# Strassen's seven products in place of eight for the second feed-forward projection, six blocks of eight, summed in DRAM

## The chip, the cores and the metric

The kernel runs on one core of one Trainium2 chip. The metric is the device time of one execution in microseconds (us). A core has five engines that run beside each other, each through its own list of instructions in order: TensorE (PE in the profile), VectorE (DVE), ScalarE (ACT), GpSimd (POOL) and SyncE (SP). Here SP and POOL only issue transfers (DMA).

## The reference

One layer of a diffusion transformer with 512 tokens and a model width of 2048. The part around the change is the feed-forward half:

```python
D_MODEL, SEQ, D_FF = 2048, 512, 8192

def sq_relu_mlp(h, w1, b1, w2, b2):
    return jnp.square(jax.nn.relu(h @ w1 + b1)) @ w2 + b2
...
    h2 = modulate(x, sh2, sc2)
    x = layer_norm(DEEPNORM_ALPHA * x + g2 * sq_relu_mlp(h2, w_ff1, b_ff1, w_ff2, b_ff2), ln2_g, ln2_b)
```

`h @ w1` is 512x2048 by 2048x8192, and the second product 512x8192 by 8192x2048. All inputs and the output are float32.

## The kernel before

The first half of the kernel (input projection, attention, convolution, output projection, first layer norm) is not touched. It leaves `h2`, transposed, and the residual stream `res[t][i]`: four tiles of 128 tokens, each in two halves of 1024 columns.

**Three matmuls for each product.** Each float32 operand is converted into a rounded high part and a low part that holds the rest (`split`): ACT writes the high part, then DVE subtracts it from the source. `mm3` multiplies high by high, high by low and low by high. A tile of weights, 128x1024, is loaded by SP into one of four tiles of `rpool` (tag `R`) and converted by `wsplit` into a pair `wh`, `wl`. The pairs live in slots that `turn["w"]` hands out in rotation, three in the feed-forward half: two of `wpool`, one of `xw`. A conversion must wait until PE is done with the slot's old weights, and for DVE's half also until ACT's half is written.

**Eight blocks.** The hidden width of 8192 is worked off in eight blocks `q` of 1024, and each block has two stages:

- the first projection, `hidden(n, ...)`, for eight groups `n` of 128 hidden columns: two tiles of weights, 48 matmuls (tile `f`), then ReLU with bias on ACT, the square on DVE, and a `split` into `fh`, `fl`. All are 512 tokens wide, except in block 0, which does the tokens in two halves.
- the second projection, `down(q, c, ...)`, for four groups `c` of 512 output columns: four tiles of weights, 96 matmuls into four PSUM banks (tile `d`, one for each 128 tokens). Then DVE multiplies each bank by the gate `g2` and adds it into `res` (`add_gated`).

```python
                for t in range(4):
                    mm3(ps[t], hi[:, s, sl], lo[:, s, sl], wh[:, s * 512:(s + 1) * 512], wl[:, s * 512:(s + 1) * 512],
                        j == j0 and s == 0, j == j1 - 1 and s == 1)
        for t in range(4):
            add_gated(g2, ps[t], t, c)
```

The hidden part is the operand that PE holds (128x128), the weights are the one that streams past it (512 columns). Block 7 does the last half of its second projection token by token, with the last layer norm and the stores behind it. The bias `b_ff2`, times the gate, is added to `res` by `bias2`, whose steps run between the groups of block 1 (`side.step`).

A scheduler sets the order of instructions on each engine when the program is built, from the order of the code, and it chooses the slots. At run time each engine keeps to its list: an instruction that waits holds up all that stand behind it on the same engine. `upool` has 30 tiles of 128x1024; 16 of them hold `h2` in the feed-forward half.

## Time and profile before

| | |
|---|---|
| time, median of 3 runs | 2460.5 us (2457.34 to 2461.24) |
| profiled execution, its own time | 2461.58 us |
| its span, first to last instruction | 2459.8 us |
| mean granted clock of TensorE | 0.996 |
| PE busy | 2405.3 us, 98% of the span, 11764 matmuls |
| DVE busy | 1368.6 us, 56% |
| ACT busy | 788.2 us, 32% |

The profile is one execution on the chip. The granted clock is the share of TensorE's full clock that the chip let it have. "Busy" counts the time in which an engine has an instruction under way; matmuls overlap their successors, so a busy PE says nothing on its pace, which is read from the starts of its matmuls. Idle time of an engine matters only where the last work to end waits for it.

### The profile page before, as it was taken

The page shows a single profiled execution, that of the slowest core. Times are in us where ns is not written, and L with a number is a line of the kernel's source. Part 1 is how long each engine was busy: PE and PEld are TensorE (multiplying, and loading weights), DVE is VectorE, ACT ScalarE, POOL GpSimd, SP SyncE. Part 2 cuts the span into 40 slices and gives each one's busy share as a digit, 9 for nine tenths or more (in the row PEclk, how much of TensorE's full clock was granted, in tenths as well). Part 3 has the DMA queues.
Part 4 walks back from the last instruction along what each step waited for, and adds up shares of the span by engine and source line. Part 5 has one row for each costly group of instructions (what it writes and reads, how often), then busy time and mean ns, then how long its engine had stood idle before and what let it go on. Part 6 is the DMA issues. An engine that isn't in the chain of part 4 may idle for free.

```text
span 2459.8 us, 29177 instructions
## 1 busy us (share of the span) xinstructions
PE 2405.3 (98%) x11764; PEld 1921.1 (78%) x11764; DVE 1368.6 (56%) x1870; ACT 788.2 (32%) x1109; POOL 51.8 (2%) x100
## 2 busy tenths in 40 slices
PE   6999999999989999999999999999999999999998
PEld 4777777777678888898888888888888888888886
DVE  4556999934767777854554433434334334334368
...
GB/s 331 243 219 188 183 221 217 278 271 263 268 207 201 166 106 199 60 155 146 120 137 94 96 99 96 95 95 94 94 95 96 101 95 94 94 94 94 98 123 106
DMA packets 109463, 371.01 MB, mean 151 GB/s; under 512 B 13064, under 2 KB 19592, under 8 KB 109328
## 3 DMA queue, kind: packets, MB, share of 16 engines
...
## 4 chain that ended last, share of the span: by engine, by line
PE 89%; issue 4%; DMA 3%; ACT 2%; DVE 2%; POOL 0%; SPq 0%; DVEq 0%; ACTq 0%; POOLq 0%
PE f L119 9%; PE f L118 9%; PE f L117 9%; PE d L119 9%; PE d L118 9%; PE d L117 9%; PE u L117 3%; PE u L118 2%; PE u L119 2%; PE gb L217 2%; PE v L117 2%; PE v L119 2%; PE v L118 2%; PE o L578 1%; PE s L556 1%
## 5 line engine op out<-in xcount | busy, mean ns | idle before, releaser
L104 DVE TENSOR_TENSOR wl<-w,wh 128x1024 fp32r<-128x1024 f32 x262 | 320.3, 1224 | 679.2 <-ACT wh L103 679.2
L103 ACT ACTIVATE wh<-w 128x1024 fp32r<-128x1024 f32 x262 | 277.3, 1060 | 901.8 <-PE d L119 502.3
L119 PE MATMUL f<-h2h,wl 128*128 128x512 f32 (+1 forms) x1152 | 424.5, 369 | 3.7 <-DVE wl L104 3.7
L117 PE MATMUL f<-h2h,wh 128*128 128x512 f32 (+1 forms) x1152 | 423.9, 368 | 0.1
L118 PE MATMUL f<-h2l,wh 128*128 128x512 f32 (+1 forms) x1152 | 423.6, 368 | 0.0
L119 PE MATMUL d<-wh,fl 128*128 128x512 f32 x960 | 379.7, 395 | 0.0
L118 PE MATMUL d<-wl,fh 128*128 128x512 f32 x960 | 376.6, 392 | 0.0
L117 PE MATMUL d<-wh,fh 128*128 128x512 f32 x960 | 374.9, 391 | 0.0
L119 PEld LDWEIGHTS f<-h2h,wl 128*128 128x128 f32 x1152 | 218.0, 189 | 41.3 <-DVE wl L104 4.3
L117 PEld LDWEIGHTS f<-h2h,wh 128*128 128x128 f32 x1152 | 218.2, 190 | 37.5 <-ACT wh L103 0.3
L118 PEld LDWEIGHTS f<-h2l,wh 128*128 128x128 f32 x1152 | 217.9, 189 | 37.2
L118 PEld LDWEIGHTS d<-wl,fh 128*128 128x128 f32 x960 | 180.3, 188 | 43.8
L117 PEld LDWEIGHTS d<-wh,fh 128*128 128x128 f32 x960 | 180.4, 188 | 40.1
L119 PEld LDWEIGHTS d<-wh,fl 128*128 128x128 f32 x960 | 180.3, 188 | 39.8
L340 DVE TENSOR_TENSOR ua<-ua,u 128x1024 f32<-128x1024 f32 x64 | 78.0, 1220 | 67.6 <-PE u L119 67.3
L117 PE MATMUL u<-hh,wh 128*128 128x512 f32 x256 | 102.9, 404 | 1.9 <-ACT hh L103 1.9
L743 DVE TENSOR_TENSOR r<-r,y 128x512 f32<-128x512 f32 x160 | 103.5, 682 | 0.2
L742 DVE TENSOR_TENSOR y<-d,g 128x512 f32<-128x512 f32 x128 | 84.8, 686 | 31.9 <-PE d L119 31.8
L118 PE MATMUL u<-hl,wh 128*128 128x512 f32 x256 | 102.1, 399 | 0.0
L119 PE MATMUL u<-hh,wl 128*128 128x512 f32 x256 | 101.3, 396 | 0.0
L280 DVE SCALAR_TENSOR_TENSOR cv<-cv,wdw 128x497 f32<-128x497 f32 (+14 forms) x120 | 89.0, 742 | 3.1
L217 PE MATMUL gb<-wb,cstat 128*32 128x512 f32 x512 | 74.2, 599 | 1.7 <-DMA wb<-in_wada_dram 1.7
...
## 6 DMA issues: line engine op xcount, KB each, us to landing
w<-in_wff_dram SPq DMA_DIRECT2D x270, 512.0 KB, 3.5
wb<-in_wada_dram SPq DMA_DIRECT2D x128, 512.0 KB, 5.5
wa<-in_wada_dram SPq DMA_DIRECT2D x64, 512.0 KB, 5.1
wu<-in_wu_dram SPq DMA_DIRECT2D x32, 512.0 KB, 8.0
k<-kd POOLq DMA_DIRECT2D x64, 192.0 KB, 5.3
wv<-in_wv_dram SPq DMA_DIRECT2D x16, 512.0 KB, 5.7
wk<-in_wk_dram SPq DMA_DIRECT2D x16, 512.0 KB, 6.5
wq<-in_wq_dram SPq DMA_DIRECT2D x16, 512.0 KB
```

The lines of the kernel that those rows point to most:

```text
L103: S.activation(hi, src, AF.Copy)
L104: V.tensor_tensor(lo, src, hi.bitcast(F32), op=ALU.subtract)
L117: T.matmul(ps, lhsT=ah, rhs=bh, start=first, stop=False)
L118: T.matmul(ps, lhsT=ah, rhs=bl, start=False, stop=False)
L119: T.matmul(ps, lhsT=al, rhs=bh, start=False, stop=last)
L217: T.matmul(gps[32 * g:32 * g + 32, 0:n], lhsT=cstat[:, kt, :], rhs=r[:, s * n:(s + 1) * n], start=kt < 4, stop=kt >= 12)
L280: V.scalar_tensor_tensor(dst[:, a:b], src[:, a + d:b + d], wdw[:, j, k:k + 1], dst[:, a:b], op0=ALU.mult, op1=ALU.add)
L340: V.tensor_tensor(uacc[j], uacc[j], ps, op=ALU.add)
L556: T.matmul(sp[:, a_:b_], lhsT=qa, rhs=ks[c][m][:, a_:b_], start=m == 0, stop=m == 1)
L578: T.matmul(ops[:, qt * P:(qt + 1) * P], lhsT=es[1][:, kk * P:(kk + 1) * P], rhs=vh[:, kk, :], start=kk == 0, stop=kk == 5)
L742: V.tensor_tensor(y[:, :512], ps, g[c // 2][:, cs_], op=ALU.mult)
L743: V.tensor_tensor(d, d, y[:, :512], op=ALU.add)
```

## The change

Blocks 0 and 7 keep the second projection as it was. In blocks 1 to 6 it is done by Strassen's scheme in the form of Winograd. The tokens (2 halves of 256), the hidden block (2 x 512) and the output columns (pairs of 2 x 512, `cp` = 0 and 1) make 2x2 blocks, and seven products `p` of half size replace eight:

- `hidden_s` makes, beside the four token-by-hidden quarters, three sums of them, and converts the quarters into `u1` and the sums into `u2`. That is four 256-wide DVE instructions and two conversions for each two groups `n`, in place of two conversions.
- The weights come in four kinds (`load_raw`: x, y, z, v), and `prep` adds them in place on DVE before converting: 8 sums and 14 conversions for each `cp`, so 16 and 28 for each block (there were 16 conversions). `LEAD = 4` conversions run ahead of PE, in four slots: two of `wpool`, two of `Pair`.
- `down_s` runs 14 steps for each `cp`, each with one converted pair and 12 matmuls into two of eight banks. Two steps make one product. ACT copies product 0 out of PSUM; DVE adds the others into four partial results `e1` to `e4` for each token tile (14 additions of 128x512 for each `cp`). `e1` and `e2` lie in a tile of `tpool`, which has two, `e3` and `e4` in the old `g1`.
- Finished partial results go to DRAM (`accd`) by POOL: plain in block 1, and with `accum_op=ALU.add` in blocks 2 to 6. That is 16 transfers of 256 KB for each block.
- The residual stream is saved to DRAM (`x1d`) in block 0, after `bias2`, which now runs there, and its tiles are used for `u1`. In block 7 `restore` reads both back and multiplies the sums by the gate.

```diff
+    x1d = [dram.tile([P, D], F32, name=f"x1d{t}") for t in range(4)]
+    accd = [dram.tile([P, D], F32, name=f"accd{t}") for t in range(4)]
...
-    def down(q, c, j0, j1, hid):
+    def down(q, c, j0, j1, hid, n=0):
+            side.step(n)
...
+    gate2()
+    side.gs = [bias2()]
+    for c in range(4):
+        down(0, c, 0, 4, hid, 2)
+        if c % 2:
+            for t in range(4):
+                nc.sync.dma_start(x1d[t][:, (c // 2) * 1024:(c // 2) * 1024 + 1024], res[t][c // 2])
+    ff.close()
...
+    st = ff.enter_context(tc.tile_pool(name="st", reuse_waits="tile", bufs=1))
+    u1 = [(unit(f"u1h{i}", (P, 4, 256), F32R), unit(f"u1l{i}", (P, 4, 256), F32R)) for i in range(4)]
+    u2 = [st.tile([P, 4, 3, 256], F32R, name=f"u2{z}") for z in "hl"]
+    class Pair:
+        def tile(self, shape, dt, tag=None, name=None):
+            return unit(name, shape, dt) if tag == "wl" else st.tile(list(shape), dt, tag="H", name=name, bufs=2)
+    turn["w"] = [wpool, Pair()]
+    def operand(p, i):
+        k = (0, 4, 5, 1, 6, 2, 3)[p]
+        if k < 4:
+            return u1[i][0][:, k, :], u1[i][1][:, k, :]
+        return u2[0][:, i, k - 4, :], u2[1][:, i, k - 4, :]
...
+        if n % 2 == 0:
+            state["ft"] = tmp(f"ft{n}", (P, 4, 256))
+        t = state["ft"]
+        tv = t[:, 2 * (n % 2):2 * (n % 2) + 2, :].rearrange("p a s -> p (a s)")
+        S.activation(tv, ps, AF.Relu, bias=bff1[:, n:n + 1])
+        V.tensor_tensor(tv, tv, tv, op=ALU.mult)
+        if n % 2:
+            i = n % 8 // 2
+            z = tmp(f"fz{n}", (P, 4, 256))
+            V.tensor_tensor(z[:, 0], t[:, 3], t[:, 1], op=ALU.subtract)
+            V.tensor_tensor(t[:, 1], t[:, 0], t[:, 1], op=ALU.subtract)
+            V.scalar_tensor_tensor(z[:, 1], z[:, 0], -1.0, t[:, 0], op0=ALU.mult, op1=ALU.subtract)
+            V.scalar_tensor_tensor(z[:, 2], z[:, 1], -1.0, t[:, 2], op0=ALU.mult, op1=ALU.subtract)
+            split(u1[i][0], u1[i][1], t)
+            split(u2[0][:, i], u2[1][:, i], z[:, 0:3])
...
+        if p == 1:
+            add(x, x, y)
+        elif p == 2:
+            add(x, x, z)
+        elif p == 3:
+            add(y, y, z)
+        elif p == 6:
+            add(v, x, v)
+        ws[cp, p, jj] = wsplit((x, x, x, y, z, v, v)[p])
+    steps = [(0, 0), (1, 0), (0, 1), (1, 1)] + [(p, jj) for p in range(2, 7) for jj in range(2)]
+    order = [(cp, p, jj) for cp in range(2) for p, jj in steps]
...
+    def store(q, e, t, c):
+        d = accd[t][:, c * 512:(c + 1) * 512]
+        if q == 1:
+            nc.gpsimd.dma_start(d, e)
+        else:
+            nc.gpsimd.dma_start(d, e, accum_op=ALU.add)
+    def down_s(q, lead):
+        ps, ev = {}, {}
+        for m, (cp, p, jj) in enumerate(order):
+            if jj == 0:
+                for t in range(2):
+                    ps[cp, p, t] = bk(f"p{q}_{cp}_{p}_{t}")
+            wh, wl = ws.pop((cp, p, jj))
+            for s in range(2):
+                i = 2 * jj + s
+                ah, al = operand(p, i)
+                for t in range(2):
+                    sl = slice(t * P, (t + 1) * P)
+                    mm3(ps[cp, p, t], ah[:, sl], al[:, sl], wh[:, s * 512:(s + 1) * 512], wl[:, s * 512:(s + 1) * 512],
+                        i == 0, i == 3)
+            if m + lead < len(order):
+                ahead(q, m + lead)
+            if jj == 0:
+                continue
+            for t in range(2):
+                b = ps[cp, p, t]
+                if p == 0:
+                    e0 = tmp(f"ev{q}_{cp}_{t}", (P, 2, 512))
+                    e1 = g1[t].rearrange("p (a s) -> p a s", a=2)
+                    ev[t] = (e0[:, 0], e0[:, 1], e1[:, 0], e1[:, 1])
+                e1, e2, e3, e4 = ev[t]
+                if p == 0:
+                    S.activation(e1, b, AF.Copy)
+                elif p == 2:
+                    V.tensor_tensor(e2, b, e1, op=ALU.add)
+                    V.tensor_tensor(e3, ps[cp, 1, t], e2, op=ALU.add)
+                elif p == 3:
+                    V.tensor_tensor(e2, b, e2, op=ALU.add)
+                    V.tensor_tensor(e4, ps[cp, 1, t], e2, op=ALU.add)
+                    store(q, e4, 2 + t, 2 * cp + 1)
+                elif p == 4:
+                    V.tensor_tensor(e3, b, e3, op=ALU.add)
+                    store(q, e3, t, 2 * cp + 1)
+                elif p == 5:
+                    V.tensor_tensor(e1, b, e1, op=ALU.add)
+                    store(q, e1, t, 2 * cp)
+                elif p == 6:
+                    V.tensor_tensor(e2, b, e2, op=ALU.add)
+                    store(q, e2, 2 + t, 2 * cp)
+    LEAD = 4
+    for q in range(1, 7):
+        for n in range(8 * q, 8 * q + 8):
+            hidden_s(n)
+            if n % 8 == 4:
+                load_raw(q, 0, 1)
+                load_raw(q, 0, 2)
+        load_raw(q, 0, 0)
+        load_raw(q, 0, 3)
+        for m in range(LEAD):
+            ahead(q, m)
+        down_s(q, LEAD)
+    ff.close()
...
+    def restore():
+        for i in range(2):
+            for t in range(4):
+                sl = slice(i * 1024, i * 1024 + 1024)
+                res[t][i] = u = unit(f"s{t}_{i}")
+                nc.sync.dma_start(u, x1d[t][:, sl])
+                a = load(accd[t][:, sl], f"ac{t}_{i}")
+                V.tensor_tensor(a[:, :512], a[:, :512], g2[i][:, :512], op=ALU.mult)
+                V.scalar_tensor_tensor(a[:, 512:], a[:, 512:], -1.0, g2[i][:, 512:], op0=ALU.mult, op1=ALU.mult)
+                V.tensor_tensor(u, u, a, op=ALU.add)
+                yield
...
+    for q in (7,):
         hid = [None] * 4
-        if q == 0:
-            turn["w"] = [wpool, wpool, xw]
-            for n in range(8):
-                if n == 4:
-                    turn["w"] = [wpool, wpool, xw, wpool, wpool, xw, wpool, Units()]
-                hidden(n, (0,), hid, n == 7)
-                side.step(4)
-            side.flush()
-            turn["w"] = [wpool, xw, wpool]
-            for n in [7, *range(7)]:
-                hidden(n, (1,), hid)
-            turn["w"] = [wpool, wpool, xw]
-            gate2()
-            side.gs = [bias2()]
-        else:
-            for n in range(8 * q, 8 * q + 8):
-                hidden(n, (0, 1), hid)
-                side.step()
-        if q < 7:
-            for c in range(4):
-                down(q, c, 0, 4, hid)
-        else:
+        turn["w"] = [wpool, wpool, xw]
+        gate2()
+        side.gs = [restore()]
+        for n in range(8 * q, 8 * q + 8):
+            hidden(n, (0, 1), hid)
+            side.step(2)
```

What the scheduler makes of it is shown at three places. The numbers behind names only tell buffers apart; `w2_2_0_1_0` is block 2, `cp` 0, kind 1 (y), half 0, and `w1_58_0` the first tile of weights of group 58.

Before, DVE at the end of the first projection of block 2: the square of the last group (23), its low part, then conversions and additions to the residual.

```order
L1053 TENSOR_TENSOR ft23_11611<-ft23_11611 128x512
L104 TENSOR_TENSOR fl11_11547<-ft23_11611,fh11_11546 128x512
L104 TENSOR_TENSOR wl_11713<-w2_2_0_3_11710,wh_11712 128x1024
L104 TENSOR_TENSOR wl_11759<-w2_2_1_0_11756,wh_11758 128x1024
L104 TENSOR_TENSOR wl_11789<-w2_2_1_1_11786,wh_11788 128x1024
L742 TENSOR_TENSOR y0_0_11740<-d2_0_0_11616,g2_0_9414 128x512
```

Now, DVE at the same place, one row earlier on. The row on `ft22` is the square of group 23 (its tile is shared by two groups).

```order
L106 TENSOR_TENSOR wl_11726<-w2_2_0_0_1_11705,wh_11725 128x1024
L1150 TENSOR_TENSOR ft22_11628<-ft22_11628 128x512
L1177 TENSOR_TENSOR w2_2_0_0_1_11705<-w2_2_0_0_1_11705,w2_2_0_2_1_11493 128x1024
L1154 TENSOR_TENSOR fz23_11694<-ft22_11628 128x256
L106 TENSOR_TENSOR wl_11745<-w2_2_0_0_0_11703,wh_11744 128x1024
L1155 TENSOR_TENSOR ft22_11628<-ft22_11628 128x256
L1156 SCALAR_TENSOR_TENSOR fz23_11694<-fz23_11694,ft22_11628 128x256
L1157 SCALAR_TENSOR_TENSOR fz23_11694<-fz23_11694,ft22_11628 128x256
L106 TENSOR_TENSOR wl_11764<-w2_2_0_0_1_11705,wh_11763 128x1024
L106 TENSOR_TENSOR u1l3_10028<-ft22_11628,u1h3_10027 128x1024
```

Between the square of group 23 and the low parts `u1l`, `u2l` that PE needs of it, there now stand one weight sum and two conversions (`w2_2_0_0_0`, `w2_2_0_0_1`, for product 2). The same rows stand in blocks 3 to 6. In block 1 DVE's rows at this place are in another order:

```order
L1150 TENSOR_TENSOR ft14_10508<-ft14_10508 128x512
L1154 TENSOR_TENSOR fz15_10574<-ft14_10508 128x256
L1155 TENSOR_TENSOR ft14_10508<-ft14_10508 128x256
L1156 SCALAR_TENSOR_TENSOR fz15_10574<-fz15_10574,ft14_10508 128x256
L1157 SCALAR_TENSOR_TENSOR fz15_10574<-fz15_10574,ft14_10508 128x256
L106 TENSOR_TENSOR u1l3_10028<-ft14_10508,u1h3_10027 128x1024
L106 TENSOR_TENSOR u2l_10030<-fz15_10574,u2h_10029 128x768
L106 TENSOR_TENSOR wl_10597<-w2_1_0_0_0_10583,wh_10596 128x1024
L106 TENSOR_TENSOR wl_10606<-w2_1_0_0_1_10585,wh_10605 128x1024
```

There the conversions for product 1 (the two rows on `w2_1_0_0_0` and `w2_1_0_0_1`) come behind the low parts of the last group.

Before, ACT in block 7, from the conversion of the first weights of group 58 on:

```order
L103 ACTIVATE wh_16617<-w1_58_0_16615 128x1024
L1052 ACTIVATE ft56_16541<-f56_0_16480,pk_100 128x512
L103 ACTIVATE fh28_16544<-ft56_16541 128x512
L103 ACTIVATE wh_16647<-w1_58_1_16645 128x1024
L103 ACTIVATE wh_16685<-w1_59_0_16683 128x1024
L1052 ACTIVATE ft57_16609<-f57_0_16548,pk_100 128x512
L103 ACTIVATE fh28_16544<-ft57_16609 128x512
L103 ACTIVATE wh_16715<-w1_59_1_16713 128x1024
L103 ACTIVATE wh_16751<-w1_60_0_16749 128x1024
```

Now, ACT in block 7, from the ReLU of group 57 on:

```order
L1055 ACTIVATE ft57_16911<-f57_0_16850,pk_108 128x512
L105 ACTIVATE fh28_16832<-ft57_16911 128x512
L105 ACTIVATE wh_16933<-w1_58_0_16931 128x1024
L105 ACTIVATE wh_16963<-w1_58_1_16961 128x1024
L105 ACTIVATE wh_17015<-w1_59_0_17013 128x1024
L105 ACTIVATE wh_17045<-w1_59_1_17043 128x1024
L1055 ACTIVATE ft58_16991<-f58_0_16930,pk_108 128x512
L105 ACTIVATE fh29_16994<-ft58_16991 128x512
L1055 ACTIVATE ft59_17073<-f59_0_17012,pk_108 128x512
L105 ACTIVATE wh_17095<-w1_60_0_17093 128x1024
```

The conversion for group 58 stood ahead of the ReLU of group 56; now it stands behind the ReLU and the high part of group 57. The one for group 60 stood two groups ahead too, and now comes behind the ReLU of group 59. On DVE the matching low parts follow the squares of groups 57 and 59.

## Rows read from the trace of the kernel before

**Rows 1.** Page, busy time, share of the span and instructions of each engine

```profile
PE 2405.3 (98%) x11764; PEld 1921.1 (78%) x11764; DVE 1368.6 (56%) x1870; ACT 788.2 (32%) x1109; POOL 51.8 (2%) x100
```

**Rows 2.** Page, chain that ended last, share of the span by engine

```profile
PE 89%; issue 4%; DMA 3%; ACT 2%; DVE 2%; POOL 0%; SPq 0%; DVEq 0%; ACTq 0%; POOLq 0%
```

**Rows 3.** Windows of block 2, first and second projection (PE, PEld, DVE, ACT, POOL busy; clock)

```profile
1388.70:1476.90 88.20, 88.20 (x386) 72.29 (x385) 31.72 (x36) 25.60 (x31) 0.00 (x0) 1.00 0.30 96
1476.90:1565.50 88.60, 88.60 (x385) 72.08 (x385) 37.59 (x46) 18.00 (x18) 0.00 (x0) 1.00 0.30 95
```

**Rows 4.** Timeline of DVE, blocks 2 and 3 (start, us, instruction, count, idle before)

```profile
1497.00 1.39 DVE L742 TENSOR_TENSOR y<-d,g 128x512 f32<-128x512 f32 x2 [1.10 <-PE d L119]
1519.17 1.38 DVE L742 TENSOR_TENSOR y<-d,g 128x512 f32<-128x512 f32 x2 [1.15 <-PE d L119]
1673.76 1.39 DVE L742 TENSOR_TENSOR y<-d,g 128x512 f32<-128x512 f32 x2 [1.10 <-PE d L119]
```

**Rows 5.** Timeline of PE, the 384 matmuls of block 2's second projection, first and next

```profile
1476.72 0.39 PE L117 MATMUL d<-wh,fh 128*128 128x512 f32 x1
...
1565.36 0.39 PE L117 MATMUL f<-h2h,wh 128*128 128x512 f32 x1
```

**Rows 6.** Groups by line and shape, 1100 to 2459 us (xcount, busy us, mean ns, idle before)

```profile
L104 DVE TENSOR_TENSOR wl<-w,wh 128x1024 fp32r<-128x1024 f32 x239 | 292.6, 1224 | 664.5 <-ACT wh L103 664.5
L103 ACT ACTIVATE wh<-w 128x1024 fp32r<-128x1024 f32 x238 | 252.3, 1060 | 882.5 <-PE d L119 502.3 <-PE f L118 371.6 <-issue 5.0
L742 DVE TENSOR_TENSOR y<-d,g 128x512 f32<-128x512 f32 x128 | 84.8, 686 | 31.9 <-PE d L119 31.8
L1053 DVE TENSOR_TENSOR ft<-ft 128x512 f32<-128x512 f32 x56 | 38.4, 685 | 0.0
L1052 ACT ACTIVATE ft<-f,pk 128x512 f32<-128x512 f32 x56 | 37.6, 672 | 0.0
L103 ACT ACTIVATE fh<-ft 128x512 fp32r<-128x512 f32 x56 | 35.4, 632 | 73.8 <-DVE ft L1053 73.8
L104 DVE TENSOR_TENSOR fl<-ft,fh 128x256 fp32r<-128x256 f32 x5 | 2.1, 424 | 1.9 <-ACT fh L103 1.9
```

**Rows 7.** Timeline of DVE, instructions that follow each other without a wait

```profile
1208.39 1.22 DVE L104 TENSOR_TENSOR wl<-w,wh 128x1024 fp32r<-128x1024 f32 x1
1209.53 1.22 DVE L1087 TENSOR_TENSOR r<-r,bf 128x1024 f32<-128x1024 f32 x1
...
1322.89 1.28 DVE L742 TENSOR_TENSOR y<-d,g 128x512 f32<-128x512 f32 x2
1324.09 1.28 DVE L743 TENSOR_TENSOR r<-r,y 128x512 f32<-128x512 f32 x2
```

**Rows 8.** Who waited for whom, 1100 to 2459 us (total us, times, longest)

```profile
ACT wh L103 <- PE d L119: 502.3, 117, 4.5
...
DVE bf L1086 <- DMA bf<-in_rows_dram: 13.0, 7, 3.7
```

**Rows 9.** Timeline of all engines, one conversion

```profile
1333.54 1.06 ACT L103 ACTIVATE wh<-w 128x1024 fp32r<-128x1024 f32 x1 [4.49 <-PE d L119]
...
1334.63 1.23 DVE L104 TENSOR_TENSOR wl<-w,wh 128x1024 fp32r<-128x1024 f32 x1 [4.32 <-ACT wh L103]
```

**Rows 10.** DMA issues (xcount, KB each, median us to landing)

```profile
w<-in_wff_dram SPq DMA_DIRECT2D x270, 512.0 KB, 3.5
k<-kd POOLq DMA_DIRECT2D x64, 192.0 KB, 5.3
kd<-ks POOLq DMA_DIRECT2D x16, 384.0 KB, 2.8
bf<-in_rows_dram SPq DMA_DIRECT2D x8, 512.0 KB, 3.8
```

**Rows 11.** Groups of POOL, 650 to 1050 us

```profile
L535 POOL DMA_DIRECT2D k<-kd x64 | 33.1, 535 | 155.3 <-PE s L556 95.4 <-DMA wq<-in_wq_dram 58.7 <-DMA k<-kd 0.7
```

**Rows 12.** Groups of DVE, the same stretch

```profile
L104 DVE TENSOR_TENSOR wobl<-wob,wobh 128x1024 fp32r<-128x1024 f32 x16 | 19.1, 1218 | 0.6 <-ACT wobh L103 0.6
```

More of the change, by code (lines that the diff above doesn't have):

```diff
@@ L854, in dit_block @@
     wk_.close()
-    spool = ctx.enter_context(tc.tile_pool(name="spool", reuse_waits="tile", bufs=6))
-    xw = ctx.enter_context(tc.tile_pool(name="xw4", reuse_waits="tile", bufs=1))
+    ff = ExitStack()
+    spool = ff.enter_context(tc.tile_pool(name="spool", reuse_waits="tile", bufs=6))
+    xw = ff.enter_context(tc.tile_pool(name="xw4", reuse_waits="tile", bufs=1))
     def bk(name):
@@ L1074, in gate2 @@
     def gate2():
+        del g2[:]
         for i in range(2):
@@ L1088, in bias2 @@
                 yield
[L1090 to L1113 removed]
+    hid = [None] * 4
@@ new lines, in dit_block @@
+    turn["w"] = [wpool, wpool, xw]
+    for n in range(8):
+        if n == 4:
+            turn["w"] = [wpool, wpool, xw, wpool, wpool, xw, wpool, Units()]
+        hidden(n, (0,), hid, n == 7)
+        side.step(4)
+    side.flush()
+    turn["w"] = [wpool, xw, wpool]
+    for n in [7, *range(7)]:
+        hidden(n, (1,), hid)
+    turn["w"] = [wpool, wpool, xw]
+    gate2()
[5 more added lines that the diff above has]
+                nc.sync.dma_start(x1d[t][:, (c // 2) * 1024:(c // 2) * 1024 + 1024], res[t][c // 2])
@@ new lines, in operand, with hidden_s @@
+    def operand(p, i):
[3 more added lines that the diff above has]
+        return u2[0][:, i, k - 4, :], u2[1][:, i, k - 4, :]
+    def hidden_s(n):
+        ps = bk(f"f{n}")
+        for j in range(2):
+            wh, wl = weights(A["wff1"][n, j], f"w1_{n}_{j}")
+            for k in range(8):
+                kt = 8 * j + k
+                bh, bl = h2k(kt, slice(0, 512))
+                mm3(ps, wh[:, k * P:(k + 1) * P], wl[:, k * P:(k + 1) * P], bh, bl, kt == 0, kt == KT - 1)
+        if n % 2 == 0:
[13 more added lines that the diff above has]
+            split(u2[0][:, i], u2[1][:, i], z[:, 0:3])
@@ new lines, in dit_block, with load_raw, prep, add @@
+    raws, ws = {}, {}
+    def load_raw(q, cp, kind):
+        for jj in range(2):
+            src = A["wff2s"][q - 1, cp, kind, jj]
+            if kind in (1, 2):
+                r = unit(f"w2_{q}_{cp}_{kind}_{jj}")
+                nc.sync.dma_start(r, src)
+            else:
+                r = load(src, f"w2_{q}_{cp}_{kind}_{jj}")
+            raws[cp, kind, jj] = r
+    def prep(q, cp, p, jj):
+        x, y, z, v = (raws[cp, k, jj] if (cp, k, jj) in raws else None for k in range(4))
+        def add(d, a, b):
+            V.tensor_tensor(d, a, b, op=ALU.add)
+        if p == 1:
[7 more added lines that the diff above has]
+        ws[cp, p, jj] = wsplit((x, x, x, y, z, v, v)[p])
@@ new lines, in dit_block, with ahead @@
+    steps = [(0, 0), (1, 0), (0, 1), (1, 1)] + [(p, jj) for p in range(2, 7) for jj in range(2)]
+    order = [(cp, p, jj) for cp in range(2) for p, jj in steps]
+    def ahead(q, m):
+        cp, p, jj = order[m]
+        prep(q, cp, p, jj)
+        if cp == 0 and jj == 1 and p == 4:
+            load_raw(q, 1, 1)
+            load_raw(q, 1, 2)
+        if cp == 0 and jj == 1 and p == 6:
+            load_raw(q, 1, 0)
+            load_raw(q, 1, 3)
+    def store(q, e, t, c):
+        d = accd[t][:, c * 512:(c + 1) * 512]
+        if q == 1:
+            nc.gpsimd.dma_start(d, e)
+        else:
+            nc.gpsimd.dma_start(d, e, accum_op=ALU.add)
@@ new lines, in dit_block @@
+    LEAD = 4
[11 more added lines that the diff above has]
+    ff.close()
+    spool = ctx.enter_context(tc.tile_pool(name="spool2", reuse_waits="tile", bufs=6))
+    xw = ctx.enter_context(tc.tile_pool(name="xw5", reuse_waits="tile", bufs=1))
@@ L1118, in dit_block @@
                 for j in (2, 3):
-                    r = load(A["wff2"][q, c, j], f"w2_{q}_{c}_{j}")
+                    r = load(A["wff2"][q // 7, c, j], f"w2_{q}_{c}_{j}")
                     for s in range(2):
@@ L1204, in _layout @@
     w2 = w_ff2.reshape(8, 4, 2, P, 4, 512)
-    o["wff2"] = c(w2.transpose(0, 4, 1, 3, 2, 5)).reshape(8, 4, 4, P, 1024)
+    o["wff2"] = c(w2[[0, 7]].transpose(0, 4, 1, 3, 2, 5)).reshape(2, 4, 4, P, 1024)
+    w2 = w2[1:7].reshape(6, 2, 2, 2, P, 2, 2, 512)
+    w2 = np.stack([w2[:, :, :, a, :, :, b] for a, b in ((0, 0), (0, 1), (1, 1), (1, 0))])
+    o["wff2s"] = c(w2.transpose(1, 5, 0, 2, 4, 3, 6)).reshape(6, 2, 4, 2, P, 1024)
     o["rows"] = c(np.stack([b_ada[2 * D:3 * D], b_ada[5 * D:6 * D], inp["b_out"][0], inp["ln1_g"][0], inp["ln1_b"][0],
```

6 lines of the change are left out of this document (4 added, 2 removed).

## The prediction

> **What bounds the kernel now.** I read the page first: PE is busy for 98% of the span [rows 1], and the chain that ended last is PE for 89% [rows 2]. The share alone could hide waits, so I read the stage that changes. In block 2, PE is busy for all of both stretches at a granted clock of 1.00, while DVE is busy for 37.6 of 88.6 us and ACT for 18.0 [rows 3]. The second projection's 384 matmuls run from 1476.72 to 1565.36 without a gap [rows 5]: 88.64 us, or 0.231 us from start to start. Blocks repeat every 176.76 us [rows 4]. DVE and ACT wait for PE there, not the reverse: ACT's conversions wait up to 4.5 us each for PE to leave a slot [rows 8]. So time here is the number of matmuls times 0.231 us, as long as PE's operands are ready.
>
> **What it removes.** Seven half-sized products are 7 x 2 x 24 = 336 matmuls for each block, each still 128x128 held and 512 columns streamed, three into one bank before the bank changes, as before. That is 48 fewer in each of six blocks, 288 in all: 288 x 0.231 = **66.5 us** if nothing waits.
>
> The section "Wait — 56ns, not 53.3ns?" of the Trainium skill's page "TensorE: Matmul & The Clock Gate" gives 215.7 ns between starts at 512 columns at 2.4 GHz; this trace has 231 ns at a granted clock of 1.00, the same level. By the page the saving would be 62.1 us; the measurement decides.
>
> **What it adds to DVE, and whether that fits.** Instructions that follow each other without a wait start 1.14 us apart at 128x1024 (1208.39, 1209.53) and 0.60 us apart at 128x512 (a pair in 1.20 us) [rows 7], each 0.08 us under its duration [rows 6]. For each `cp` there are 14 conversions and 8 weight sums at 1.14 and 14 additions out of PSUM at 0.60, so 33.5 us, against 14 steps of 12 x 0.231 = 2.77 us on PE, 38.8 us. DVE fills 86% of the stage. ACT has 14 x 1.06 us [rows 6] and two copies. Both fit, but a pair needs ACT (1.06), then DVE 0.03 us later [rows 9], and a sum ahead of it needs DVE first; ACT must also wait for PE to leave the slot. So I followed DVE's rows from `cp` 0 to `cp` 1, the densest place, with the end of product 3 as zero. Additions of product 3, one conversion and two sums fill DVE to 5.3; products 4 and 5, three conversions and two sums to 14.1; then two conversions, product 6 and two sums to 19.9. The conversion for step 3 of `cp` 1 is done at 21.1 (PE wants it at 25.4), that for step 5 at 27.2 (wanted at 31.0). The least slack is 3.7 us, and I take no stall there. In the first projection DVE has some 40 us of work (16 conversions, 8 squares, and for each two groups four 256-wide instructions and two conversions), hidden behind 88 us of PE.
>
> **Where PE does wait.** Three places follow from the order rows. A matmul lasts 0.39 us and the next starts 0.23 us after it [rows 5], so others can go on some 0.2 us after PE has gone on to the next step. Times are from the start of the first product, in block 7 from the end of the group named.
> - *Blocks 2 to 6, start of the products.* ACT's high part for step 3 needs the slot that the last group held, so it runs 0.2 to 1.3 and the ReLU (0.67, [rows 6]) behind it to 2.0. DVE: conversion to 2.4, square to 3.0, weight sum to 4.2, one 256-wide instruction (0.42 in [rows 6], less 0.08) to 4.5, conversion to 5.7, three 256-wide to 6.7. The next conversion needs the slot of step 1 (5.54): ACT to 6.8, DVE to 8.0. Only then comes `u1l`, ready at 9.2. PE wants it in the second half of step 2, at 5.54 + 1.39, third matmul, 7.4. Late by 1.8 us, five times: 9.0 us.
> - *Block 1.* DVE does square, four 256-wide instructions, `u1l` and `u2l` first, to 6.5, and the conversion for step 1 after them, to 7.7. PE wants it at 2.77 + 0.46 = 3.2. Late by 4.4 us.
> - *Block 7.* `restore` takes tiles of `rpool` that the weights also use, and the conversion for group 58 stands behind ReLU (0.2 to 0.9), square (1.5) and high part (0.63, to 2.2) of group 57: ACT to 3.2, DVE to 4.5, where PE wants the low part 0.46 after the group's start. Late by 4.0 us. Group 60 stands behind the ReLU of 59 alone: ACT to 1.9, DVE to 3.2, late by 2.8 us.
>
> Together 20.2 us. What gets late next is only what hangs on PE: the conversions behind follow PE's steps and keep their lead.
>
> **What I cost at nothing.** Weight bytes are the same, 16 tiles for each block. x and v of `cp` 1 load only when those of `cp` 0 are free, at 4.2 on the scale above; with 3.5 us to land [rows 10] they arrive at 7.7, and the first conversion can start at 8.4. `bias2` moves from block 1 to block 0's second projection: 19 us of DVE, with bias rows that land in 3.8 us [rows 10] and had DVE waiting 13.0 us over 7 times [rows 8], under 88.6 us of matmuls. With two bias rows for each tile of weights in the four `rpool` tiles, I find the fourth conversion 2 us early; were that cover gone, 0 to 3 us. The saves of `x1d` block SP until DVE's additions are done, with four loads ahead. The end is unchanged.
>
> **Accumulating transfers.** The trace has none. The tile with `e1` and `e2` is wanted back by ACT's copy in the next `cp`. The store of product 6 is issued at 17.2, and the copy may start at 27.9 before the conversion behind it on ACT makes PE late, so 10.6 us may pass. POOL spends 0.53 us to issue one [rows 11]. The nearest rows: a store to DRAM by POOL lands in 2.8 us, a load in 5.3 [rows 10]. Below, 2.8; above, twice the load, 10.6, as an estimate for one read and one write of the destination. I take some 6, between the store that it mostly is and that end: no stall. DVE's conversions beside POOL's issues took 1.22 us [rows 12], as elsewhere, so I add nothing for that.
>
> The section on the bandwidth ceiling in the Trainium skill's page "Collectives: The Full Stack" says that adding in the transfer costs two source reads in place of one, about halving the rate. By that a store of 2.8 us becomes 5.6; no run here shows it yet, and the sum is the same.
>
> **The sum.** 2461.6 (the profiled execution's own time; its span is 1.8 us shorter) - 66.5 + 20.2 = 2415.3. That execution was 1.1 us above the median of 2460.5, so I predict **2415 us**, with 2405 to 2427 for this case (0 to 30 us of waits).
>
> **Rivals.**
> - *Nothing waits.* The waits at block starts vanish if slots come free earlier than I read them: 2461.6 - 66.5 = 2395. Against it: the orders are fixed lists. Chance 0.12.
> - *The conversions' hand-over binds.* If each of the 16 sums of a block holds DVE for ACT's 1.06 us as well, DVE needs 67.0 + 17 = 84 us against 77.5 of matmuls: 6.5 us for each block, 39 in all, 2454; half of it, 2435. For it: before, DVE waited 664.5 us for ACT's high parts [rows 6]. Against it: those were waits for PE's slots, and the new rows put other work between a sum and its conversion. Chance 0.14 for 2427 to 2455, 0.04 for no measurable change.
> - *The transfers hold back the products.* Each us that an accumulating transfer needs beyond 10.6 stalls ACT's copy, and PE with it, in six blocks: 6 us in all. The gain of 46.3 is gone at 10.6 + 46.3 / 6 = 18.3 us. At 25 us: 2415 + 86 = 2501, slower than before. For it: four of them (1 MB, read twice) come within 8 us beside loads of weights. Against it: transfers average 95 GB/s in this stage [rows 3]. Chance 0.10.
>
> **Chances and range.** The forecast has 0.60. A measurement of this kernel tells changes of about 0.2% (5 us) from none. Faster 0.60 + 0.12 + 0.14 = 0.86, no change 0.04, slower 0.10. The range 2395 to 2440 leaves out the slow transfers and the worse half of the hand-over.
>
> **What would show it.** PE with 11476 matmuls, pitch 0.231 in the products, and gaps of 2 us at the start of five blocks, 4 in block 1, 4 and 3 in block 7, each behind ACT or DVE. Accumulating transfers landing under 10 us. I am wrong if PE's pieces inside the products wait for DVE, if ACT waits for a POOL transfer, or if the products' matmuls start further apart than 0.231 us.

## The result, and the profile after

The changed kernel takes **2421.6 us** (median of 4 runs, 2419.51 to 2423.28); the kernel before, beside it, 2460.87 us (2457.34 to 2461.88). The ratio is 0.9844, 95% interval 0.9831 to 0.9856. Predicted were 2415 us and 2395 to 2440. The profiled execution took 2423.28 us, its span 2421.5 us.

The page of the changed kernel: busy time, and the chain that ended last.

```profile
PE 2351.7 (97%) x11476; PEld 1868.9 (77%) x11476; DVE 1615.8 (67%) x2136; ACT 884.1 (37%) x1205; POOL 128.9 (5%) x196
PE 85%; DVE 5%; DMA 5%; ACT 3%; issue 1%; SPq 0%; POOL 0%; DVEq 0%; ACTq 0%
```

PE has 288 matmuls fewer than in [rows 1]. Its share of the chain fell from 89% [rows 2], and DVE and transfers took what it gave up, so PE now waits somewhere. The windows by stage say where (block 0 second projection; block 1 first and products; block 3 first and products; block 7 first projection; columns as in [rows 3]).

```profile
1122.70:1213.20 90.50, 89.22 (x387) 72.01 (x386) 52.52 (x61) 17.76 (x18) 0.00 (x0) 1.00 0.50 168
1213.20:1302.30 89.10, 89.10 (x385) 71.87 (x384) 43.69 (x52) 28.30 (x32) 0.00 (x0) 1.00 0.38 136
1302.30:1381.60 79.30, 78.03 (x337) 62.94 (x336) 67.67 (x75) 33.82 (x35) 7.60 (x14) 1.00 0.37 132
1547.70:1636.20 88.50, 88.50 (x385) 72.13 (x384) 43.45 (x50) 27.13 (x30) 2.41 (x3) 1.00 0.42 132
1636.20:1713.90 77.70, 77.70 (x338) 62.94 (x337) 63.72 (x71) 32.89 (x35) 11.98 (x14) 1.00 0.53 124
2212.60:2321.50 108.90, 94.94 (x385) 74.98 (x384) 53.75 (x60) 26.55 (x31) 1.73 (x2) 0.94 0.63 193
```

The products have no gap left to find: 77.7 us, all of it PE at a clock of 1.00, with DVE busy for 63.7. One stage stands out: the first projection of block 7 takes 108.9 us, 14.0 of them idle, where the same matmuls took 88.0 before, and its clock is 0.94.

Starts of PE's stages, before and after, make the balance. Each line is a stage's length less its length before; for products, less 77.56, which is 336/384 of the 88.64 in [rows 5].

| stage | lost, us | predicted |
|---|---|---|
| block 0, second projection (88.65 to 90.46) | 1.8 | 0 (0 to 3) |
| block 1, first projection (87.99 to 89.14) | 1.2 | 0 |
| block 1, products (79.28) | 1.7 | 4.4 |
| blocks 2 to 6, first projections (442.46 in place of 440.18) | 2.3 | 0 |
| blocks 2 to 6, products (388.54 in all) | 0.7 | 9.0 |
| block 7, first projection (87.99 to 108.91) | 20.9 | 6.8 |
| together | 28.6 | 20.2 |

66.5 - 28.6 = 37.9; the work ahead of block 0's second projection was 0.7 us shorter and the tail 0.3 longer, which gives the 38.3 us between the spans.

**Block 7.** Timelines of SP, DVE, ACT and PE at its start, as issued and as waited for:

```profile
2200.64 1.46 SPq L724 DMA_DIRECT2D bg<-in_rows_dram  x2
2203.47 1.47 SPq L101 DMA_DIRECT2D w<-in_wff_dram  x2
2213.40 2.92 SPq L101 DMA_DIRECT2D ac<-accd  x2
2216.42 0.85 SPq L1082 DMA_DIRECT2D g<-g1d  x2
2225.64 2.95 SPq L101 DMA_DIRECT2D w<-in_wff_dram  x2
...
2224.39 1.22 DVE L1084 TENSOR_TENSOR g<-g,bg 128x1024 f32<-128x1024 f32 x1 [7.23 <-DMA g<-g1d]
...
2229.88 1.06 ACT L105 ACTIVATE wh<-w 128x1024 fp32r<-128x1024 f32 x1 [15.17 <-DMA w<-in_wff_dram]
...
2230.99 0.80 PE L119 MATMUL f<-h2h,wh 128*128 128x512 f32 x1 [6.80 <-ACT wh L105]
2249.19 0.72 PE L119 MATMUL f<-h2h,wh 128*128 128x512 f32 x1 [4.56 <-ACT wh L105]
2275.00 0.50 PE L119 MATMUL f<-h2h,wh 128*128 128x512 f32 x1 [1.72 <-ACT wh L105]
```

Read it backwards. PE waits 6.80 us for the high part of group 57's weights, ACT 15.17 us for their load, and SP issues that load only at 2225.64. Before it in SP's list stand four loads: two `ac`, and two gate rows `g`. The two `bg` and two `ac` tiles fill `rpool`; the first is free again when DVE has used it, and DVE sits 7.23 us on the gate row. Groups 58 and 60 follow late in the same way. So part of what the page's chain gives to DVE, DMA and ACT is this one mechanism: with the later restore of experiment 1 the page has 3%, 3% and 2% for them, in place of 5%, 5% and 3%.

The idle 14.0 us is not all of it. PE's matmuls after the first two gaps last 0.80 and 0.72 us, against 0.39 in [rows 5], and the granted clock of the stretch after the first gap is:

```profile
2230.00:2250.00 20.00, 14.41 (x50) 10.66 (x50) 13.21 (x16) 6.19 (x8) 0.00 (x0) 0.84 0.77 252
```

PE ran part of it at the lower of its two levels, 1.2 GHz, after 6.8 us of idleness. The stage's busy time is 94.9 us for work that took 88.0, so 6.9 of the 20.9 us are clock, not waiting.

**Start of the products.** Timelines of DVE and PE in block 2, whose products start at 1470.10:

```profile
1478.07 1.22 DVE L106 TENSOR_TENSOR u1l<-ft,u1h 128x1024 fp32r<-128x1024 f32 x1
...
1476.96 0.39 PE L119 MATMUL p<-wh,u2h 128*128 128x512 f32 x1
...
1477.90 0.50 PE L119 MATMUL p<-wh,u1h 128*128 128x512 f32 x1
...
1479.16 0.40 PE L121 MATMUL p<-wh,u2l 128*128 128x512 f32 x1
1479.39 0.68 PE L121 MATMUL p<-wh,u1l 128*128 128x512 f32 x2
```

`u1l` is done at 1479.29, 9.2 us after the start, as predicted to a tenth. But PE was not there at 7.4. Its list in the built program, up to the matmuls on that low part (`p2_0_0` is product 0, `p2_0_1` product 1 of block 2; the last number is the bank, other numbers are left out):

```
L119 MATMUL p2_0_1_0<-wh,u2h
L120 MATMUL p2_0_1_0<-wl,u2h
L121 MATMUL p2_0_1_0<-wh,u2l
L119 MATMUL p2_0_1_1<-wh,u2h
L119 MATMUL p2_0_0_0<-wh,u1h3
L120 MATMUL p2_0_0_0<-wl,u1h3
L119 MATMUL p2_0_0_1<-wh,u1h3
L120 MATMUL p2_0_0_1<-wl,u1h3
L120 MATMUL p2_0_1_1<-wl,u2h
L121 MATMUL p2_0_1_1<-wh,u2l
L121 MATMUL p2_0_0_0<-wh,u1l3
L121 MATMUL p2_0_0_1<-wh,u1l3
```

The scheduler had put six matmuls of product 1, and two of the other bank, ahead of the first that needs `u1l`. That one comes 40 matmuls after the start (40 x 0.231 = 9.2 us), not 32, and PE meets it without a wait.

Block 1, whose products start at 1302.32, shows the same. PE's timeline at the place where step 1 wants its low part:

```profile
1307.98 0.73 PE L121 MATMUL p<-wh,u1l 128*128 128x512 f32 x2
1309.98 0.50 PE L120 MATMUL p<-wl,u2h 128*128 128x512 f32 x1 [1.27 <-DVE wl L106]
```

26 matmuls stand ahead of the first that needs that low part, so PE comes there some 6.0 us after the start (26 x 0.231), not at 3.2.

**Accumulating transfers.** POOL's groups and the transfers' landing (KB each, median us):

```profile
L1207 POOL DMA_DIRECT2D accd<-ev x40 | 34.3, 910 | 92.3 <-DVE ev L1247 51.0 <-DVE ev L1250 39.9 <-DVE wl L106 1.2
L1205 POOL DMA_DIRECT2D accd<-ev x8 | 4.3, 540 | 14.9 <-DVE ev L1250 8.1 <-DVE ev L1247 6.4 <-issue 0.2
...
accd<-g POOLq DMA_DIRECT2D x48, 256.0 KB, 7.8
accd<-ev POOLq DMA_DIRECT2D x48, 256.0 KB, 5.4
```

An accumulating issue (L1207) holds POOL for some 0.9 us where a plain one (L1205) holds it 0.54. The landing is below 10 us in the median, and ACT's copies waited 4.2 us for it in all, in four places.

### The profile page after: what moved, and what is told of

Its sections match the earlier page's. It is cut to its first block, busy times and chain, and to the rows that moved or that the text cites. A ratio compares the mean times of both kernels' runs of the same rounds, so it can differ in the third digit from the quotient of the medians.

```text
span 2421.5 us, 29325 instructions
## 1 busy us (share of the span) xinstructions
PE 2351.7 (97%) x11476; PEld 1868.9 (77%) x11476; DVE 1615.8 (67%) x2136; ACT 884.1 (37%) x1205; POOL 128.9 (5%) x196
## 4 chain that ended last, share of the span: by engine, by line
PE 85%; DVE 5%; DMA 5%; ACT 3%; issue 1%; SPq 0%; POOL 0%; DVEq 0%; ACTq 0%
PE f L121 9%; PE f L119 9%; PE f L120 9%; PE p L120 6%; PE p L119 6%; PE p L121 6%; PE gb L219 2%; PE u L119 2%; PE u L120 2%; PE u L121 2%; PE v L119 2%; PE d L121 2%; PE d L120 2%; PE d L119 2%; PE o L580 1%; DVE wl L106 1%
## 5 line engine op out<-in xcount | busy, mean ns | idle before, releaser
L106 DVE TENSOR_TENSOR wl<-w,wh 128x1024 fp32r<-128x1024 f32 x334 | 404.0, 1221 | 398.2 <-ACT wh L105 397.8
L105 ACT ACTIVATE wh<-w 128x1024 fp32r<-128x1024 f32 x334 | 351.3, 1059 | 753.5 <-PE f L120 305.7
L119 PE MATMUL p<-wh,u1h 128*128 128x512 f32 x384 | 151.5, 395 | 0.0
L120 PE MATMUL p<-wl,u1h 128*128 128x512 f32 x384 | 150.8, 393 | 0.0
L121 PE MATMUL p<-wh,u1l 128*128 128x512 f32 x384 | 149.9, 393 | 0.0
L1177 DVE TENSOR_TENSOR w<-w,w 128x1024 f32<-128x1024 f32 x96 | 115.8, 1217 | 0.8
L120 PE MATMUL p<-wl,u2h 128*128 128x512 f32 x288 | 113.4, 394 | 1.3 <-DVE wl L106 1.3
L121 PE MATMUL p<-wh,u2l 128*128 128x512 f32 x288 | 112.9, 392 | 0.0
L119 PE MATMUL p<-wh,u2h 128*128 128x512 f32 x288 | 112.8, 392 | 0.0
L119 PEld LDWEIGHTS p<-wh,u1h 128*128 128x128 f32 x384 | 72.0, 188 | 17.9 <-ACT u1h L105 1.5
```

Source lines behind the costliest of these rows:

```text
L105: S.activation(hi, src, AF.Copy)
L106: V.tensor_tensor(lo, src, hi.bitcast(F32), op=ALU.subtract)
L119: T.matmul(ps, lhsT=ah, rhs=bh, start=first, stop=False)
L120: T.matmul(ps, lhsT=ah, rhs=bl, start=False, stop=False)
L121: T.matmul(ps, lhsT=al, rhs=bh, start=False, stop=last)
L1177: V.tensor_tensor(d, a, b, op=ALU.add)
```

## The experiments

The first four kernels change the kernel after; those of experiments 5 to 8 change the one of the first experiment, and those of 9 to 11 add to that of experiment 7.

**1. Block 7: restore later.** The gate rows and `restore` come two groups later and in smaller steps.

```diff
-        gate2()
-        side.gs = [restore()]
         for n in range(8 * q, 8 * q + 8):
             hidden(n, (0, 1), hid)
-            side.step(2)
+            if n % 8 == 1:
+                gate2()
+                side.gs = [restore()]
+            side.step(2 if n % 8 > 5 else 1)
```

> In block 7 the gate rows are loaded after group 57 in place of before group 56, and the restore of the residual takes one step for each group (two in the last two). Theory A (the gate rows load late, two of the four tiles of rpool are held for them, and the weights of group 57 stand behind them in SP's order): the first projection of block 7 falls from 108.9 us to 88 to 93, the time from 2421.6 to 2401 to 2407. Rival B (it is the 8 MB that restore reads beside the weights, 193 GB/s in this stage, wherever they stand): the same bytes cost the same, the stage stays above 103 us and the time above 2416.

Measured: 2400.67 us (2399.6 to 2403.52), ratio 0.9764 (0.9748 to 0.9781).

**2. Block 7: the sums read into other tiles.**

```diff
-                a = load(accd[t][:, sl], f"ac{t}_{i}")
+                a = unit(f"ac{t}_{i}")
+                nc.sync.dma_start(a, accd[t][:, sl])
```

> In block 7 the sums read back from DRAM land in tiles of upool, not of rpool; gate rows and restore stay where they are. Theory A, in the form that the tiles of rpool and what stands ahead of the weights of group 57 decide: those weights are then ahead of the gate rows and of restore on SP, the stage falls from 108.9 us to 90 to 97, the time to 2403 to 2410. Rival B (bytes): stage above 103, time above 2416. If this kernel stays slow and the one with the later restore is fast, it is the place of the loads and not the tiles.

Measured: 2403.06 us (2400.36 to 2404.27), ratio 0.9769 (0.9755 to 0.9784). The stage is below the 90 to 97 us that theory A gave for it. Windows of block 7's first projection, experiment 1 and then experiment 2:

```profile
2210.20:2298.20 88.00, 88.00 (x386) 72.10 (x385) 49.58 (x58) 25.54 (x30) 2.53 (x3) 1.00 0.69 216
2214.40:2302.50 88.10, 88.10 (x386) 72.08 (x385) 52.36 (x60) 25.96 (x32) 1.73 (x2) 1.00 0.71 238
```

No gap is left in either, though transfers now move 216 and 238 GB/s in place of 193. The same bytes cost nothing, so the rival of the bytes is out. SP's timeline of experiment 2 narrows theory A too:

```profile
2205.29 12.44 SPq L101 DMA_DIRECT2D w<-in_wff_dram  x4
2217.82 0.86 SPq L1082 DMA_DIRECT2D g<-g1d  x2
```

The gate rows are issued at 2217.82, later than the 2216.42 of the kernel after, and PE waits for nothing. A late gate row is harmless in this order. What cost 20.9 us is that the weights of group 57 stood behind it and behind `ac`, on SP and in `rpool`. Both experiments change the order on SP; what the shared tiles of `rpool` would cost without it, no run separates.

**3. Plain stores.**

```diff
-            nc.gpsimd.dma_start(d, e, accum_op=ALU.add)
+            nc.gpsimd.dma_start(d, e)
```

> All partial results are stored plainly, without adding, so the sum over blocks 1 to 6 is left out and only block 6 counts. Theory: accumulating transfers stay inside the 10.6 us that they have, so the time stays within 3 us of 2421.6, the products at 77.6 us for each block; only the landing (5.4 and 7.8 us) and POOL's issue (0.855 us) fall, to 3 to 5 us and some 0.54 us. Rival: adding in the transfer costs something where the trace doesn't name it (the 0.45 us by which each first projection of blocks 2 to 6 is longer, the copies of ACT that wait): 3 to 10 us faster.

Measured: 2418.54 us (2414.89 to 2420.05), ratio 0.9832 (0.9817 to 0.9846), 3.1 us less, on the edge between the theory (within 3) and the rival (3 to 10). The two places that the rival names are out: the first projections stay at 88.49 and the products of blocks 2 to 6 at 77.6 each. The whole gain is in block 7's first projection, 105.5 us in place of 108.9, where SP now issues the weights of group 57 at 10.1 us from the stage's start, in place of 13.0. Landing of the transfers of blocks 2 to 6 alone (those of block 1 are plain in both kernels), in the kernel after and then in this run:

```profile
accd<-g POOLq DMA_DIRECT2D x40, 256.0 KB, 8.1
accd<-ev POOLq DMA_DIRECT2D x40, 256.0 KB, 6.0
...
accd<-g POOLq DMA_DIRECT2D x40, 256.0 KB, 4.9
accd<-ev POOLq DMA_DIRECT2D x40, 256.0 KB, 4.2
```

So adding costs 1.8 us of landing for one kind and 3.2 for the other, a factor of 1.4 and 1.6, and 0.3 to 0.4 us of POOL, none of it on the path of the products. The section on the bandwidth ceiling in the Trainium skill's page "Collectives: The Full Stack" had the second source read halve the rate. It says so of the reduce step in a ring of cores, not of a store to DRAM; this case shows a smaller loss in the same direction, and in the time to landing, which is not a rate.

**4. DVE overfilled.** In `prep`'s `add`:

```diff
             V.tensor_tensor(d, a, b, op=ALU.add)
+            V.tensor_tensor(d, d, d, op=ALU.max)
```

> Each of the 8 weight sums of a cp is followed by one more 128x1024 instruction on DVE (the maximum of the sum with itself, which changes no value). Theory (DVE's fill is 33.5 of 38.8 us, and it binds when it is over): 33.5 + 8 x 1.14 = 42.6 us, 3.8 us over for each of 12 cp, 46 us slower, 2460 to 2475 with what is lost at the starts. Rival hand-over (each instruction in a sum's chain also holds DVE for ACT's 1.06 us): 8 x 1.06 more for each cp, 100 us further, 2530 to 2570. Rival slack (leads and the first projection take it up): under 15 us slower.

Measured: 2462.24 us (2455.86 to 2464.55), ratio 1.0009 (0.9999 to 1.0019): 40.6 us slower than the kernel after, which is the whole gain. From the start of one block's products to the next it is 174.8 to 175.9 us for blocks 2 to 5, in place of 166.1 to 166.4. That is 8.7 to 9.4 more; the fill says 2 x 3.8 = 7.6. In the profiled execution blocks 1 to 6 take 45.0 us more than in the kernel after, where the theory had 46, and block 7's first projection 5.7 us less. The rival that charges the hand-over too is out by 68 us at the least.

**5. Each store twice**, on top of experiment 1 (`acc2` is declared like `accd`; block 1's plain stores are doubled too).

```diff
             nc.gpsimd.dma_start(d, e, accum_op=ALU.add)
+            nc.gpsimd.dma_start(acc2[t][:, c * 512:(c + 1) * 512], e, accum_op=ALU.add)
```

> On the kernel with the later restore (2400.7 us): each partial result goes to DRAM twice, the second time to a second set of tiles that nobody reads. Theory (a budget of 10.6 us from the issue of product 6's store to the copy that reuses the tile; the single transfer needs 5.4 us in the median): the pair needs 8 to 13 us, so at most 2.4 us of stall for each of the 6 changes of cp inside a block, 0 to 14 us in all, 2400 to 2415, and ACT's copies of product 0 are what waits. Rival (the transfers are at their limit already, ACT's copies having waited up to 1.3 us for them): each us more stalls PE, 3 to 6 us at each change, 2419 to 2437.

Measured: 2422.33 us (2420.18 to 2424.43), ratio 0.9847 (0.9832 to 0.9862): 21.7 us slower than experiment 1, more than the theory's 14 and inside the rival's range. The products of blocks 2 to 6 take 85.1, 81.8, 79.8, 79.7 and 80.2 us. ACT's and PE's timelines in block 2:

```profile
1526.95 0.60 ACT L1238 ACTIVATE ev<-p 128x512 f32<-128x512 f32 x1 [11.77 <-DMA acc<-ev]
...
1528.54 0.79 PE L120 MATMUL p<-wh,u2h 128*128 128x512 f32 x1 [4.03 <-ACT wh L106]
```

Place and mechanism are the predicted ones: the copy waits for the transfer, and the conversion behind it on ACT makes PE late. The copy came 33.1 us after the end of product 3 (1471.64 + 8 x 2.77), PE lost 4.2, so it may come at 28.9; the prediction had 27.9. The other end of the budget was wrong: product 6's stores are issued 20.2 and 21.9 us after that point in the kernel after (1512.46 and 1514.19), not at 17.2. So the first has 8.7 us, not 10.6. POOL's timelines, in the kernel after and in this run (the last store that the copy waits for):

```profile
1512.46 0.85 POOL L1207 DMA_DIRECT2D accd<-ev  x1 [3.16 <-DVE ev L1250]
...
1516.14 0.85 POOL L1210 DMA_DIRECT2D acc<-ev  x1 [0.20 <-issue]
```

A single transfer of this tile, landing in 4.5 to 5.5 us at this place, fits. Of the pair, the first is issued at 1515.09 and the second at 1516.14, and the copy can start only at 1526.95, 11.9 us after the first issue.

**6. Half the extra work for DVE**, on top of experiment 1: the added maximum only behind the sums of products 1 and 2.

```diff
             add(x, x, y)
+            V.tensor_tensor(x, x, x, op=ALU.max)
         elif p == 2:
             add(x, x, z)
+            V.tensor_tensor(x, x, x, op=ALU.max)
```

> On the kernel with the later restore (2400.7 us): four extra 128x1024 instructions on DVE for each cp, behind the sums of products 1 and 2, where the run before had eight. Theory of the fill: 33.5 + 4 x 1.14 = 38.1 of 38.8 us, 98%, not over, so only the places with little slack lose something: 0 to 3 us for each block, 2401 to 2419. Rival (each extra instruction costs its 1.14 us as soon as DVE is this full, since conversions come in bursts): 4 x 1.14 x 12 = 55 us, 2440 to 2455; half the loss of the run with eight (about 20 us, 2421) would lie between.

Measured: 2415.68 us (2414.61 to 2417.32), ratio 0.9822 (0.9806 to 0.9838): 15 us slower than experiment 1, in the theory's range. At 98% full, DVE makes each block's products 2 to 4 us longer, and PE waits in them for DVE's conversions (8.2 us, ten times). So the last 5 us of room in a `cp` can't all be used. That conversions for PE come due in bursts is the likely reason, not one that was tried apart: the added instruction also stands between a sum and its conversion and makes that chain 1.14 us longer.

**7. The output bias spread**, on top of experiment 1.

```diff
-    down(0, c, 0, 4, hid, 2)
+    down(0, c, 0, 4, hid, 1)
```

> The later restore, and one step of the output bias for each tile of weights in block 0 in place of two. Theory: the two waits of PE in block 0 (0.5 and 0.5 to 1.1 us, behind DVE's conversions) go, its second projection falls from 89.9 to 88.7 us, the time from 2400.7 to 2399.5, which is within the spread of the runs. Rival (the bias work delays the save of the residual and so block 1): no gain in the sum of blocks 0 and 1.

Measured: 2399.86 us (2398.94 to 2402.74), ratio 0.9758 (0.9743 to 0.9772). Block 0's second projection takes 88.65 us, as before the change, in place of 89.86; block 1 is as it was. The time can't show 1.2 us, the stage does.

**8. The low part later**, on top of experiment 1: two more instructions on DVE between `u1h` and `u1l` of each block's last groups.

```diff
+            S.activation(u1[i][0], t, AF.Copy)
+            if n % 8 == 7:
+                V.tensor_tensor(t, t, t, op=ALU.max)
+                V.tensor_tensor(t, t, t, op=ALU.max)
+            V.tensor_tensor(u1[i][1], t, u1[i][0].bitcast(F32), op=ALU.subtract)
-            split(u1[i][0], u1[i][1], t)
```

> The later restore, and two more 128x1024 instructions on DVE (a maximum of the tile with itself, which changes no value) ahead of the low part u1l of each block's last groups, so that it is ready some 2.3 us later, 11.5 us after the start of the products. In PE's list the scheduler has now put the matmuls on that low part 14 rows further back, behind those of the product after. Theory (PE's list bends around late operands, which is why the predicted waits did not come): no more than 0.5 us for each block, 2399 to 2404. Rival (order by products, as the prediction had it: wanted at 7.4 us): 4.1 us late in each block, 24 us in all, 2420 to 2428.

Measured: 2405.85 us (2400.91 to 2406.71), ratio 0.9776 (0.9761 to 0.979), 1.9 us above the theory's range and far below the rival's. In block 2, whose products start at 1467.73, DVE finishes `u1l` at 1480.18, 12.5 us after the start; PE's timeline there:

```profile
1480.04 0.40 PE L120 MATMUL p<-wl,u2h 128*128 128x512 f32 x1
1480.28 0.69 PE L121 MATMUL p<-wh,u1l 128*128 128x512 f32 x2
```

No gap: the two matmuls now stand after product 2's first ones. The products of blocks 2 to 6 are 77.63 to 78.17 us, 1.1 us more in all, where order by products would have cost some 20. Only block 1 has a new wait, 3.25 us for `u1l`, and its products take 82.8 us in place of 79.3: there the list did not bend far enough, which is what the theory missed.

**9 to 11. Fewer slots in the first projections**, on top of experiment 7. Experiment 9 uses `[wpool, wpool, pair]` there, experiment 10 `[wpool]`, as shown; `pair` is the old `Pair()`. Experiment 11 sets `[wpool]` in block 7's first projection too.

```diff
     for q in range(1, 7):
+        turn["w"] = [wpool]
         for n in range(8 * q, 8 * q + 8):
             hidden_s(n)
...
+        turn["w"] = [wpool, pair]
         load_raw(q, 0, 0)
```

> On the kernel with the later restore and the spread bias (2399.9 us): in the first projections of blocks 1 to 6 the converted weights rotate through three slots (two of wpool, one of the new pair), as the kernel before did, in place of four; the products keep four. Theory (which slots two tiles that follow each other lie in sets the pace of PE: before, every third group of 48 matmuls took 10.91 us and the others 11.04 to 11.07; with four slots all take 11.05 to 11.08): each first projection falls from 88.49 to 87.9 to 88.2 us, with every third group at 10.91. Rival (something else of the stage, transfers or DVE's added work, slows it): it stays at 88.4 to 88.5. Either way the time moves by 3 us at the most, unless the start of the products gets new waits.

> The same with two slots, both of wpool. Theory of the slots: every group has the same pair, so all eight groups of a first projection last the same, within 0.02 us, and the stage is 88.0 us or less, or 88.5, and not between. Rival: groups stay as with four slots, 11.05 to 11.08, and the stage 88.4 to 88.5, which alone would not tell the two apart; only together with the run with three slots does it.

> The best pieces together, timed: the later restore, the spread bias, and two slots, both of wpool, in the first projections of blocks 1 to 7. The single look at the kernel with two slots in blocks 1 to 6 gave 2393.3 us. Theory of the slots: block 7's first projection falls from 88.01 to 87.1 us as the others did, the time to 2391 to 2394, ratio to the kernel before 0.972 to 0.974. Rival (in block 7, with restore's transfers beside the weights, two slots leave the conversions too little lead): the stage gets waits and stays at 88 us or more, the time at 2393 to 2400.

Measured: experiment 9, 2402.56 us (2398.92 to 2404.21), ratio 0.9766 (0.975 to 0.9783), not told apart from experiment 7; experiment 10, a single run, 2393.28 us; experiment 11, 2394.13 us (2391.17 to 2394.54), ratio **0.9725** (0.9712 to 0.9739), the fastest of those that ran more than once. PE's starts of block 3's first projection (in experiment 9 of its first four groups) and of the products behind it, with three slots and then with two (384 matmuls each):

```profile
1546.20 0.40 PE L119 MATMUL f<-h2h,wh 128*128 128x512 f32 x1
...
1557.12 0.40 PE L119 MATMUL f<-h2h,wh 128*128 128x512 f32 x1
...
1568.18 0.39 PE L119 MATMUL f<-h2h,wh 128*128 128x512 f32 x1
...
1579.21 0.39 PE L119 MATMUL f<-h2h,wh 128*128 128x512 f32 x1
...
1634.17 0.39 PE L119 MATMUL p<-wh,u1h 128*128 128x512 f32 x1
```

```profile
1544.38 0.40 PE L119 MATMUL f<-h2h,wh 128*128 128x512 f32 x1
...
1631.46 0.39 PE L119 MATMUL p<-wh,u1h 128*128 128x512 f32 x1
```

That is 87.97 us with three slots, 87.08 with two, and 88.49 with four, at a clock of 1.00 and without a gap in each. With two slots, groups of 48 matmuls last 10.88 us (the first 10.92). With three, the first, fourth and seventh group, whose two pairs of tiles both lie in `wpool`, last 10.90 to 10.92 and the other five, with one pair elsewhere, 11.03 to 11.06, as the theory had it from the kernel before. With four, every group has one pair in `Pair`, and all last 11.06 or 11.07. It is not the number of tiles: `Pair` has two high parts of its own (`bufs=2`), so experiment 9 has as many as the change and uses those of `Pair` less often. The change made eight such groups out of five, 3 x 0.16 = 0.5 us for each block, so the 2.3 us in the first projections of blocks 2 to 6 came with the slots, and the change could have gained there. In experiment 11 block 7's stage falls from 88.01 to 87.08 as well.

Block 1 pays for it. In experiment 9 its two stages took 90.28 and 81.87 us in place of 89.11 and 79.25, which is more than that run gained elsewhere. With two slots the first takes 87.05, but the products 81.9 (experiment 10) and 84.0 (experiment 11), with a wait of 2.3 us for `u1h` near their start.

## Why the prediction was right, and where it was not

**Right: what bounds the kernel, and the 66.5 us.** The products run at 77.63 to 77.95 us a block, 0.231 us a matmul, as in [rows 5]. DVE's fill was right in kind: it leaves no stall at 33.5 us for each `cp`, costs 15 us in all at 38.1 and the whole gain at 42.6 (experiments 6 and 4). Neither the hand-over nor the transfers cost what their rivals said, and the waits did not vanish as the first rival had it.

**Right by cancelling: the 20.2 us of waits.** They were 28.6, from other places.

- *Block 7, the step that was mis-sized:* 6.8 predicted, 20.9 measured. ReLU ahead of the conversion was the wrong queue. The prediction read ACT's and DVE's lists, took "what gets late next" as nothing, and left out SP's list, where the weights of group 57 stand behind `ac` and `g`. It had no price for the gate rows either: the first let DVE go 8.0 us after its issue, and the second landed after 10.1. Moving the loads, or giving `ac` other tiles, brings the stage to 88.0 and 88.1 (experiments 1 and 2). The lower clock after the gaps, 6.9 us, had no term at all.
- *Blocks 2 to 6, the step that failed:* `u1l` was ready at 9.2 as worked out, but "PE wants it at 7.4" came from the order of products in the code and not from PE's own list. 9.0 predicted, 0.7 measured. Experiment 8 shows the list bending further.
- *Block 1:* the conversion for step 1 was done 7.6 us after the start, against 7.7 predicted; PE waited 1.54 us there, not 4.4. The stage lost 1.7. The list hid the rest: PE came there at 6.0, not at the 3.2 of the order of products. That is read from the trace; no run tried it.
- *Block 0:* 1.8 us, within the 0 to 3 given; experiment 7 removes it.
- *First projections of blocks 1 to 6, a term put at nothing:* 3.5 measured. The prediction asked only whether DVE's work fits, and took PE's pace as unchanged by the new slots; experiments 9 to 11 show that it isn't.

So 2415 is near 2421.6 by luck: 14.1 us too little in block 7, and 5.3 too little in block 0 and the first projections, stand against 11.0 too much at the starts of the products.

**Right with a wrong budget: the transfers.** They landed in 5.4 and 7.8 us, under the 10 named, without a stall. But the 10.6 us were 8.7, since product 6's stores are issued 3 us later than worked out, and experiment 5 overran them. The rival's break-even of 18.3 us was too generous by the same 1.9 us.

**Open.** Why block 1's first projection takes 1.2 us more than before: 0.5 of it is what the other blocks lost to the slots, and with two slots the stage takes 87.05 us. And which property of the tiles outside `wpool` slows PE.
